# Two experts in 32 slots, and the last expert's rows added to the sums by VectorE

## The chip, the cores and the metric

The kernel runs on one core of a Trainium2 chip. The metric is device microseconds of one execution. TensorE (PE, with PEld its weight loads) multiplies, VectorE (DVE) and ScalarE (ACT) work element by element, GpSimd (POOL) issues indirect and small DMAs, SyncE (SP) issues the weight loads. A difference of under about 0.2% can't be told from no change.

## What is computed

Two layers of a token mixer followed by a channel mixer, on 256 latent and 256 context tokens of 1024 features, in float32. The second layer's channel mixer is the part in question: each of 256 tokens goes to its best two of eight experts.

```python
def moe_swiglu(h, router, w1, w3, w2):
    logits = (h @ router).astype(jnp.float32)
    top_vals, top_idx = lax.top_k(logits, TOP_K)        # TOP_K = 2
    top_w = jax.nn.softmax(top_vals, axis=-1)
    gates = jnp.sum(jax.nn.one_hot(top_idx, N_EXPERTS, dtype=jnp.float32) * top_w[..., None], axis=-2)
    out = jnp.zeros_like(h)
    for e in range(N_EXPERTS):                          # w1, w3: 1024 x 2816; w2: 2816 x 1024
        out = out + gates[..., e:e + 1].astype(h.dtype) * swiglu(h, w1[e], w3[e], w2[e])
    return out
```

Here swiglu(h, w1, w3, w2) is (silu(h @ w1) * (h @ w3)) @ w2. Its sum is normalised, multiplied by a gate and added to the tokens: the output.

## The kernel before

The trunk (first layer, second layer's token mixer) is not touched by the change. The experts run in `experts`, in the order of RUNS (line 35), each on a fixed number of token slots, SLOTS (line 33). Position 0 is always expert 0; positions 1 to 7 are the other experts by falling load (lines 1499 to 1513). An expert with more tokens than slots is finished in a loop behind the output (line 1605), under a condition that is false as long as all tokens fit.

An expert's weights are 33 tiles of 128 x 2048 float32, 1 MiB each: in `up` six chunks of up to 512 columns of w1 and w3 (four tiles a chunk, the last chunk of 256 columns two), in `down` eleven tiles of w2. `wload` (line 164) issues them on SP's queue, in the order of use, into a rotating set of 13 buffers; before the first expert starts, six more tiles go to memory lent by other buffers. A tile is issued when the buffer before it in the rotation has been read.

Products come in two kinds. A group of 128 slots splits each weight tile on ScalarE and VectorE into a high and a low part (`wsplit`, line 175) and uses three fast products for one (`mm3`, line 232). A smaller group of m slots uses plain float32 products, which the trace records as two each, with the group's features as the stationary operand, m columns wide, and 128/m such products on different column groups of the array (lines 1336 to 1341 and 1365 to 1369). For 64 slots a product of `up` has 256 weight columns and two column groups, for 32 slots 128 and four; in `down` 512 and two, or 256 and four. In the chunk of 256 columns both forms have 128 columns and two column groups. Behind each chunk `act` multiplies the two halves and transposes the result on TensorE (line 1306), once per 128 columns of it.

While a run computes, `ready` prepares the next: `index` finds the tokens by a small product (line 1223), `fetch` gets their rows by an indirect DMA from `xrows`, which was stored at line 1544 in run 0, and `gather` transposes them (line 1278). Each step of it is placed behind one more chunk. `scatter` writes an expert's results to `yrows`. For the last run it is different: its results don't go through memory. `add_up` reads all others' results back and adds them; `last_sums` loads these sums into four PSUM banks by a product with the identity (line 1394); `combine` scales the last expert's results, splits them and adds them to the same banks by products with a one-hot matrix; `output` reads the banks.

Of the kernel before, what the change touches and what calls it, by code (L numbers as in the profile page):

```python
# [10 lines left out]
F32 = mybir.dt.float32  # L11
F32R = mybir.dt.float32r
I32 = mybir.dt.int32
AF = mybir.ActivationFunctionType
OP = mybir.AluOpType
# [14 lines left out]

SLOTS = (64, 160, 128, 128, 64, 64, 64, 64)

RUNS = ((0,), (2,), (4,), (1, 6), (5,), (3,), (7,))
SCRATCH = 4096
RING2, RING3 = 3, 6
MA = 3
# [7 lines left out]
def shape_constants():  # L46
# [5 lines left out]
    c[:, C_I8:C_I8 + 8] = np.arange(8)  # L52
    c[:, C_CAP:C_CAP + 8] = SLOTS
    p = np.arange(128)
# [27 lines left out]
def finish(steps):  # L82
    for _ in steps:
        pass
# [12 lines left out]
class Net:  # L97
# [1059 lines left out]
    def experts(self, pool):  # L1157
        nc, I = self.nc, self.I
        v = nc.vector
# [3 lines left out]
        onesr = pool.tile([128, 128], F32R, name="onesr", tag="G", bufs=1)  # L1163
        tri = pool.tile([128, 128], F32R, name="tri", tag="GT", bufs=1)
        v.tensor_copy(onesr, self.ones)
# [23 lines left out]
        for t in range(2):  # L1189
            for s in range(t + 1):  # L1190
                nc.tensor.matmul(p[:, t * 8:t * 8 + 8], lhsT=tri if s == t else onesr, rhs=sel[:, s],
                                 start=s == 0, stop=s == t)
# [8 lines left out]
        pieces = []  # L1201
# [55 lines left out]
            return xr, few  # L1257

        def group(n):
            return pool.tile([128, 4, 8 * n], F32, name="few", tag=f"few{n}", bufs=1 + n // 64)  # L1260

        def gather(base, n, rk=None, w=None, got=None):

            xr, few = got or (None, None)
            if xr is None:
                P = places("P", base, n, rk, w, 1)
            if n < 128:
                few = few or group(n)
                xs = few[:, 0].rearrange("p (k s) -> p k s", s=n)
            else:  # L1270
                xh = pool.tile([128, KB, 128], F32R, name="xh", tag="xh", bufs=1)
                xl = pool.tile([128, KB, 128], F32R, name="xl", tag="xl", bufs=1)
            for q in range(2):
                p = self.at()
                for k in range(4):
                    d = (4 * q + k) * 128
                    if xr is not None:
                        nc.tensor.transpose(p[:, k * 128:k * 128 + n], xr[:, d:d + 128], self.ident[:n, :n])
                        continue
                    for t in range(2):  # L1280
                        nc.tensor.matmul(p[:, k * 128:k * 128 + n], lhsT=res[t][:, d:d + 128], rhs=P[:, t, :n],
                                         start=t == 0, stop=t == 1)
                xg = xs[:, 4 * q:4 * q + 4] if n < 128 else pool.tile([128, 4, 128], F32, name="xg", tag="xg", bufs=1)
                for k in range(4):
                    kk = 4 * q + k
                    a, b = A[:, 0, kk:kk + 1], B[:, 0, kk:kk + 1]
                    if q:
                        nc.scalar.activation(xg[:, k, :n], p[:, k * 128:k * 128 + n], AF.Identity, scale=a, bias=b)
                    else:
                        v.tensor_scalar(xg[:, k, :n], p[:, k * 128:k * 128 + n], a, b, op0=OP.mult, op1=OP.add)  # L1290
                s = slice(4 * q, 4 * q + 4)
                if n == 128:
                    self.split(xh[:, s], xl[:, s], xg)
            return (xh, xl) if n == 128 else (xs, few)
# [79 lines left out]
                                     f + j == 0, f + j == FB - 1)  # L1374
                yield ys

        def adder(base, n, rk, gt_, last=False):

            p = self.at()
            G = places("G", base, n, rk, None, 1)  # L1380
            for t in range(2):
                nc.tensor.transpose(p[:, t * 128:(t + 1) * 128], G[:, t], self.ident)
            for t in range(2):
                nc.tensor.matmul(p[:, 256:257], lhsT=G[:, t], rhs=gt_(t), start=t == 0, stop=t == 1)
            GT = pool.tile([128, 256], F32R, name="GT", tag="GT", bufs=1)
            nc.scalar.activation(GT, p[:, :256], AF.Copy)
            gcol = pool.tile([128, 1], F32, name="gcol", tag="gcol", bufs=2)
            v.tensor_copy(gcol, p[:, 256:257])
            sums = []
            if last:  # L1390

                sums = [self.at() for _ in pieces]
                for o, a in zip(sums, pieces):
                    nc.tensor.matmul(o, lhsT=self.ident, rhs=a, start=True, stop=False)
            return n, GT, gcol, sums

        def combine(to, y):
            n, GT, gcol, sums = to

            parts = []  # L1400
            ys = pool.tile([128, 4, 512], F32R, name="ys", tag="acts", bufs=MA)
            for i, h in enumerate(y):
                hi, lo = ys[:, 2 * i], ys[:, 2 * i + 1]
                nc.scalar.activation(hi, h, AF.Copy, scale=gcol)
                v.scalar_tensor_tensor(lo, h, gcol, hi.bitcast(F32), op0=OP.mult, op1=OP.subtract)
                parts.append((hi, lo))
            for t in range(2):
                for half in range(2):
                    o = sums[2 * t + half] if sums else self.at()
                    r = slice(0, 128) if n == 128 else slice(64 * half, 64 * half + 64)  # L1410
                    for i, x in enumerate(parts[half % len(parts)]):
                        nc.tensor.matmul(o, lhsT=GT[r, t * 128:(t + 1) * 128], rhs=x[r], start=i == 0 and not sums, stop=i == 1)
                    a = pieces[2 * t + half]
                    if not sums:
                        v.tensor_add(a, a, o)

        def weights(e, static):
            def at_(name):
# [5 lines left out]
        def ready(pos, t):  # L1424


            ns = [min(128, SLOTS[pos] - b) for b in range(0, SLOTS[pos], 128)]
            t[pos] = ns, [], []
# [12 lines left out]
        def last_gate():  # L1441
            g = pool.tile([128, D], F32, name="fgate", tag="xh", bufs=1)
            s = self.gscr[1, 1, 0]
            nc.gpsimd.dma_start(g, bass.AP(tensor=s.tensor, offset=s.offset, ap=[[0, 128], [1, D]]))
            return g

        def output(outs, src, g):
            for t in range(2):
                ss = self.small.tile([128, 1, 2], F32, name="ss", tag="ss", bufs=6)
                for half in range(2):  # L1450
                    c = slice(half * 512, half * 512 + 512)
                    junk = pool.tile([128, 512], F32, name="junk", tag="mg", bufs=2)
                    nc.scalar.activation(junk, src[2 * t + half], AF.Square, accum_out=ss[:, 0, half:half + 1])
                    v.tensor_mul(outs[2 * t + half], src[2 * t + half], g[:, c])
                r = self.scale(ss, D)
                for half in range(2):
                    c = slice(half * 512, half * 512 + 512)
                    v.scalar_tensor_tensor(outs[2 * t + half], outs[2 * t + half], r, res[t][:, c], op0=OP.mult, op1=OP.add)
                    nc.sync.dma_start(self.out[t * 128:(t + 1) * 128, c], outs[2 * t + half])
# [13 lines left out]

        def last_sums():
            pos, = RUNS[-1]
            return adder(0, SLOTS[pos], lambda t: rankp[:, t, pos:pos + 1], lambda t: gatep[:, t, pos:pos + 1], True)

        cur = {}
        first_w = lambda t: w0[:, t:t + 1]
# [2 lines left out]
        with self.behind(self.latest(DVE, ACT)):  # L1482
# [5 lines left out]
            for i in range(2):  # L1488
                o, m, b = sm([128, 2, NE], f"oh{i}"), sm([128, 2, NE], f"ohl{i}"), sm([128, 2], f"best{i}")
# [37 lines left out]
            rankp, gatep = sm([128, 2, NE], "rankp"), sm([128, 2, NE], "gatep")  # L1527
# [28 lines left out]

        for i, run in enumerate(RUNS):
            if i == 1:
                n_over = nc.values_load(overi[0:1, NE:NE + 1], min_val=0, max_val=SEQ)
            if i == len(RUNS) - 1:  # L1560
                fgate = last_gate()
            ups, w2s = [], []
            for pos in run:
                ns, xs, _ = cur[pos]
# [7 lines left out]
            nxt = {}  # L1572
            side = chain(*(ready(pos, nxt) for pos in RUNS[i + 1])) if i + 1 < len(RUNS) else add_up()

            hold = self.behind([] if i else routed)
            for c, aTs in enumerate(zip(*ups)):
# [3 lines left out]
                else:  # L1580
                    hold.close()
                    if i == 0:
                        cur[0][2].append(index(0, 0, SLOTS[0])[1:])
            finish(side)
            last = i == len(RUNS) - 1
            if last:
                to = last_sums()
# [10 lines left out]
        outs = pool.tile([128, 4, 512], F32, name="outs", tag="few64", bufs=2)  # L1598
        outs = [outs[:, i] for i in range(4)]

        output(outs, to[-1], fgate)
        for a, o in zip(pieces, to[-1]):
            nc.scalar.activation(a, o, AF.Copy)

        with self.tc.If(n_over > 0):
            with self.tc.For_i(0, NE, 1) as e:
                n_e = nc.values_load(overi[0:1, bass.ds(e, 1)], min_val=0, max_val=SEQ)
                for base in (0, 128):
                    with self.tc.If(n_e > base):
# [4 lines left out]
                        rk = lambda t: col[:, 0, t]  # L1614
# [145 lines left out]
```

## Time and profile before

| | us |
|---|---|
| median of 3 runs (lowest, highest) | 1521.48 (1519.68, 1522.76) |
| the profiled execution, its own time | 1520.14 |
| its span, first to last instruction | 1517.9 |
| TensorE busy | 1452.5 |
| the experts, first up-product to last down-product | 804 to 1502 |

The stages of the experts, from the order of instructions: run 0 (position 0, 64 slots) 804 to 872.6, run 1 (position 2, 128 slots) to 975, run 2 (position 4, 64) to 1046, run 3 (positions 1 and 6, 128 + 32 and 64) to 1259, run 4 (position 5, 64) to 1330, run 5 (position 3, 128) to 1432.5, run 6 (position 7, 64) to 1502, then the output to 1518. Busy time counts an engine's instructions; it doesn't say who waits for whom. The page's granted clock is a share of TensorE's full 2.4 GHz; 1.2 GHz is the other level.

### The profile page before, as it was taken

What the parts mean: (1) busy time and instruction counts of PE and PEld (TensorE: products, weight loads), DVE (VectorE), ACT (ScalarE), POOL (GpSimd) and SP (SyncE); (2) the same over time, 40 slices, a digit from 0 to 9 for tenths busy, and PEclk for the clock granted to TensorE, in tenths of its full rate; (3) what the DMA queues carried; (4) which work ended last, traced back from release to release, by engine and by line L of the source; (5) the groups of instructions that cost most, each with busy time, mean ns of one, the idle gap of its engine ahead of it and who ended that gap; (6) DMA issues with size and microseconds to landing.
All of it is one profiled execution on the core that took longest, in us unless ns stands there. A gap on an engine that the chain in (4) does not pass through costs nothing.

```text
span 1517.9 us, 22725 instructions
## 1 busy us (share of the span) xinstructions
PE 1452.5 (96%) x9006; PEld 1053.9 (69%) x9007; DVE 823.6 (54%) x1551; ACT 616.4 (41%) x983; POOL 62.5 (4%) x93
## 2 busy tenths in 40 slices
PE   7999999999999999999998999999999998999996
PEld 5677667988878888788665477764666655477762
DVE  3496687774554545778763088622454341078612
ACT  4336654423222222456641177522343331177511
POOL 1010200000000001000000010000000001010000
PEclk9999999999999999999999999999999999999998
DMA  8773223344453525353379899999998899999994
GB/s 340 278 285 146 86 98 123 141 170 163 142 206 135 207 100 186 119 186 111 118 293 420 351 416 368 370 403 419 419 355 329 326 363 393 420 421 409 409 420 180
DMA packets 62995, 410.82 MB, mean 271 GB/s; under 512 B 9428, under 2 KB 10136, under 8 KB 15648
## 3 DMA queue, kind: packets, MB, share of 16 engines
q1 hardware_dynamic: 54864, 392.19, 66.1%
q0 software_dynamic: 5616, 16.29, 2.9%
q8 instruction: 73, 1.20, 0.3%
q10 hardware_dynamic: 2400, 0.79, 0.2%
q14 instruction: 42, 0.34, 0.1%
HBM read 402.27 MB, written 6.98 MB: 270 GB/s over the span
## 4 chain that ended last, share of the span: by engine, by line
PE 84%; DVE 6%; DMA 5%; ACT 3%; issue 2%; ACTq 0%; POOL 0%; DVEq 0%; POOLq 0%
PE mm L1339 12%; PE mm L236 11%; PE mm L235 11%; PE mm L237 11%; PE mm L1368 7%; PE at L235 7%; PE at L236 7%; PE at L237 6%; PE md L373 1%; PE at L747 1%; DVE whl L162 1%; DMA more<-yrows 1%; DMA xr<-xrows,src 1%; PE at L724 1%; DMA few<-xrows,src 1%
## 5 line engine op out<-in xcount | busy, mean ns | idle before, releaser
L162 DVE TENSOR_TENSOR whl<-w,whl 128x1024 fp32r<-128x1024 f32 x310 | 374.5, 1223 | 267.6 <-ACT whl L161 259.2
L161 ACT ACTIVATE whl<-w 128x1024 fp32r<-128x1024 f32 x310 | 323.7, 1058 | 294.0 <-PE at L237 174.1
L1339 PE MATMUL mm<-w,few 128*64 128x256 f32 (+2 forms) x2528 | 225.8, 347 | 0.0
L1339 PEld LDWEIGHTS mm<-w,few 128*64 128x64 f32 (+1 forms) x2528 | 147.6, 133 | 68.6 <-issue 17.7
L1368 PE MATMUL mm<-w,few 128*64 128x512 f32 (+1 forms) x616 | 111.2, 536 | 0.0
L235 PE MATMUL mm<-hh,whl 128*128 128x512 f32 (+1 forms) x256 | 95.7, 374 | 1.2 <-ACT hh L161 1.2
L236 PE MATMUL mm<-hl,whl 128*128 128x512 f32 (+1 forms) x256 | 95.9, 375 | 0.0
L237 PE MATMUL mm<-hh,whl 128*128 128x512 f32 (+1 forms) x256 | 95.5, 373 | 0.0
L1368 PEld LDWEIGHTS mm<-w,few 128*64 128x64 f32 (+1 forms) x616 | 35.0, 129 | 70.6 <-issue 68.3
L237 PE MATMUL mm<-whl,hl 128*128 128x256 f32 (+1 forms) x240 | 80.9, 342 | 0.0
L236 PE MATMUL mm<-whl,hh 128*128 128x256 f32 (+1 forms) x224 | 75.3, 338 | 1.8 <-DVE whl L162 1.8
L1303 DVE TENSOR_TENSOR mg<-mg,mm 128x256 f32<-128x256 f32 (+2 forms) x36 | 13.6, 378 | 114.2 <-ACT mg L1302 114.2
L235 PE MATMUL mm<-whl,hh 128*128 128x256 f32 (+1 forms) x224 | 74.8, 338 | 0.0
L236 PE MATMUL at<-hl,whl 128*128 128x512 f32 (+1 forms) x192 | 71.3, 371 | 0.0
L237 PE MATMUL at<-hh,whl 128*128 128x512 f32 (+1 forms) x192 | 71.3, 371 | 0.0
L235 PE MATMUL at<-hh,whl 128*128 128x512 f32 (+1 forms) x192 | 71.2, 371 | 0.0
L367 DVE SCALAR_TENSOR_TENSOR wsum<-w,sc,wsum 128x1024 f32<-128x1024 f32 x48 | 59.7, 1281 | 20.8 <-DMA w<-in_w_mod_dram 20.8
L1302 ACT ACTIVATE mg<-mm 128x256 f32<-128x256 f32 (+3 forms) x54 | 22.8, 422 | 117.7 <-PE mm L1339 113.1
L235 PE MATMUL mm<-whl,xh 128*128 128x512 f32 (+1 forms) x144 | 57.9, 402 | 7.5 <-ACT whl L161 7.5
L236 PE MATMUL mm<-whl,xh 128*128 128x512 f32 (+1 forms) x144 | 57.2, 397 | 2.8 <-DVE whl L162 2.8
L235 PEld LDWEIGHTS mm<-hh,whl 128*128 128x128 f32 x256 | 48.2, 188 | 11.3 <-issue 2.1
L237 PE MATMUL mm<-whl,xl 128*128 128x512 f32 (+1 forms) x144 | 55.6, 386 | 0.0
(492 smaller groups left out, 2604.1 us busy)
## 6 DMA issues: line engine op xcount, KB each, us to landing
w<-in_moe_w_dram SPq DMA_DIRECT2D x258, 1024.0 KB, 11.5
w<-in_w_mod_dram SPq DMA_DIRECT2D x48, 1024.0 KB, 6.0
w<-in_ffn_w_dram SPq DMA_DIRECT2D x33, 1024.0 KB, 4.9
w<-in_w_in_dram SPq DMA_DIRECT2D x16, 1024.0 KB, 4.9
w<-in_w_out_dram SPq DMA_DIRECT2D x8, 1024.0 KB, 5.5
wa<-in_moe_w_dram SPq DMA_DIRECT2D x3, 1024.0 KB, 9.7
gate<-gscr POOLq DMA_DIRECT2D x5, 512.0 KB, 4.8
band<-in_band_dram SPq DMA_DIRECT2D x4, 512.0 KB, 7.8
```

The lines of the kernel that those rows point to most:

```text
L161: self.nc.scalar.activation(hi, x, AF.Copy)
L162: self.nc.vector.tensor_sub(lo, x, hi.bitcast(F32))
L235: mm(out, lhsT=a[0], rhs=b[0], start=start, stop=False)
L236: mm(out, lhsT=a[0], rhs=b[1], start=False, stop=False)
L237: mm(out, lhsT=a[1], rhs=b[0], start=False, stop=stop)
L367: nc.vector.scalar_tensor_tensor(x, y, c, x, op0=OP.mult, op1=OP.add)
L373: nc.tensor.matmul(p[32 * j:32 * j + 32], lhsT=self.sc[:, k], rhs=w[:, 0, j * 512:(j + 1) * 512], start=k == split, stop=k == KB - 1 and n ...
L724: nc.tensor.matmul(sp[:, :n], lhsT=qT[:, h, t * 128:t * 128 + 128], rhs=kT[:, kv, j, c0:], start=j == 0, stop=j == 1)
L747: nc.tensor.matmul(op[64 * i:64 * i + 64, side * 256:side * 256 + 256], lhsT=vt[:, b + 2 * side, kv * 64:kv * 64 + 64], rhs=src[:, b], sta ...
L1302: nc.scalar.activation(s1[:r, :c], h1[:r, :c], AF.Silu)
L1339: nc.tensor.matmul(h[i][m * j:m * j + m, :c], lhsT=x[0][:, k], rhs=t[:, k - k0, j * c:j * c + c], start=k == 0, stop=k == KB - 1, tile_pos ...
L1368: nc.tensor.matmul(y[0][m * q:m * q + m, :c], lhsT=x[0][:, b], rhs=w[:, j, c * q:c * q + c], start=f + j == 0, stop=f + j == FB - 1, tile_ ...
```

## The change

SLOTS gives 32 slots instead of 64 to positions 0 and 7. RUNS pairs position 7 instead of 6 with position 1 in run 3, and position 6 instead of 7 runs last. The 32-slot buffers (`few32`) become two; the scratch tile of a 128-row gather takes its memory from the ring of `mg` instead of one of its own. In the last run the sums stay in SBUF: `combine` scales the results in two halves, ScalarE one and VectorE the other, places them by one plain float32 product for each of four output blocks instead of two split ones, and VectorE adds each block to the sums. `output` then reads the sums, and four copies behind it are gone.

```diff
-SLOTS = (64, 160, 128, 128, 64, 64, 64, 64)
-RUNS = ((0,), (2,), (4,), (1, 6), (5,), (3,), (7,))
+SLOTS = (32, 160, 128, 128, 64, 64, 64, 32)
+RUNS = ((0,), (2,), (4,), (1, 7), (5,), (3,), (6,))
...
-            return pool.tile([128, 4, 8 * n], F32, name="few", tag=f"few{n}", bufs=1 + n // 64)
+            return pool.tile([128, 4, 8 * n], F32, name="few", tag=f"few{n}", bufs=2)
...
-                xg = xs[:, 4 * q:4 * q + 4] if n < 128 else pool.tile([128, 4, 128], F32, name="xg", tag="xg", bufs=1)
+                xg = xs[:, 4 * q:4 * q + 4] if n < 128 else pool.tile([128, 4, 128], F32, name="xg", tag="mg", bufs=2)
...
-            GT = pool.tile([128, 256], F32R, name="GT", tag="GT", bufs=1)
+            GT = pool.tile([128, 256], F32, name="GT", tag="GT", bufs=1)
...
-            sums = []
-            if last:
-                sums = [self.at() for _ in pieces]
-                for o, a in zip(sums, pieces):
-                    nc.tensor.matmul(o, lhsT=self.ident, rhs=a, start=True, stop=False)
-            return n, GT, gcol, sums
+            return n, GT, gcol
...
-            parts = []
-            ys = pool.tile([128, 4, 512], F32R, name="ys", tag="acts", bufs=MA)
+            ys = pool.tile([128, 2, 512], F32, name="ys", tag="acts", bufs=MA)
             for i, h in enumerate(y):
-                hi, lo = ys[:, 2 * i], ys[:, 2 * i + 1]
-                nc.scalar.activation(hi, h, AF.Copy, scale=gcol)
-                v.scalar_tensor_tensor(lo, h, gcol, hi.bitcast(F32), op0=OP.mult, op1=OP.subtract)
-                parts.append((hi, lo))
+                nc.scalar.activation(ys[:, i, :256], h[:, :256], AF.Copy, scale=gcol)
+                v.tensor_scalar(ys[:, i, 256:], h[:, 256:], gcol, None, op0=OP.mult)
             for t in range(2):
                 for half in range(2):
-                    o = sums[2 * t + half] if sums else self.at()
+                    o = self.at()
                     r = slice(0, 128) if n == 128 else slice(64 * half, 64 * half + 64)
-                    for i, x in enumerate(parts[half % len(parts)]):
-                        nc.tensor.matmul(o, lhsT=GT[r, t * 128:(t + 1) * 128], rhs=x[r], start=i == 0 and not sums, stop=i == 1)
+                    nc.tensor.matmul(o, lhsT=GT[r, t * 128:(t + 1) * 128], rhs=ys[r, half % len(y)], start=True, stop=True)
                     a = pieces[2 * t + half]
-                    if not sums:
-                        v.tensor_add(a, a, o)
+                    v.tensor_add(a, a, o)
...
-        output(outs, to[-1], fgate)
-        for a, o in zip(pieces, to[-1]):
-            nc.scalar.activation(a, o, AF.Copy)
+        output(outs, pieces, fgate)
```

## Rows read from the trace of the kernel before

**Rows 1.** The page: busy time and share of the span by engine.
```profile
PE 1452.5 (96%) x9006; PEld 1053.9 (69%) x9007; DVE 823.6 (54%) x1551; ACT 616.4 (41%) x983; POOL 62.5 (4%) x93
```

**Rows 2.** By stretch: us, PE, PEld, DVE, ACT, POOL busy, clock, DMA share, GB/s.
```profile
804.00:872.60 68.60, 64.93 (x500) 36.07 (x499) 13.05 (x69) 11.84 (x27) 1.77 (x2) 0.98 0.94 382
872.60:975.00 102.40, 99.66 (x454) 78.94 (x454) 87.30 (x88) 76.44 (x84) 4.07 (x2) 0.98 0.99 389
...
1046.00:1259.00 213.00, 208.76 (x1823) 135.13 (x1825) 93.28 (x101) 81.26 (x109) 4.96 (x3) 0.99 0.94 363
1259.00:1330.00 71.00, 64.84 (x497) 36.04 (x493) 5.95 (x18) 8.06 (x20) 3.81 (x4) 0.95 1.01 411
...
798.00:1502.00 704.00, 676.74 (x4782) 444.71 (x4782) 304.64 (x426) 269.11 (x361) 25.51 (x20) 0.98 0.97 385
```

**Rows 3.** Whom TensorE waited for, 804 to 1502: us in total, times, longest.
```profile
PE at L1278 <- DMA xr<-xrows,src: 7.9, 2, 5.1
PE mm L235 <- ACT whl L161: 7.5, 4, 2.3
PE at L1306 <- DVE mg L1303: 5.5, 5, 2.7
...
```

**Rows 4.** Whom SP's queue waited for, 804 to 1502.
```profile
SPq L172 <- PE mm L1339: 206.2, 97, 12.7
```

**Rows 5.** Busy time by stretch, columns as in rows 2: the last loads.
```profile
1490.00:1500.00 10.00, 10.00 (x48) 3.31 (x46) 0.00 (x0) 0.00 (x0) 0.00 (x0) 1.00 0.36 147
```

**Rows 6.** Timeline of TensorE: start, us, then the instruction; 32-slot and 64-slot up-products.
```profile
1059.21 1.08 PE L1339 MATMUL mm<-w,few 128*32 128x128 f32 x32
1060.22 0.50 PE L235 MATMUL at<-whl,xh 128*128 128x512 f32 x1
...
1441.71 7.13 PE L1339 MATMUL mm<-w,few 128*64 128x256 f32 x64
1448.77 0.44 PE L1306 MATMUL at<-cst,mg 128*128 128x128 f32 x2
...
1475.84 1.97 PE L1339 MATMUL mm<-w,few 128*64 128x128 f32 x32
```

**Rows 7.** Timeline of TensorE: the 64-slot down-products of run 0.
```profile
853.38 19.10 PE L1368 MATMUL mm<-w,few 128*64 128x512 f32 x88
```

**Rows 8.** Groups by form, run 3: count, busy us, mean ns, idle before.
```profile
L1339 PE MATMUL mm<-w,few 128*32 128x128 f32 x704 | 29.1, 282 | 0.0
...
L1368 PE MATMUL mm<-w,few 128*32 128x256 f32 x176 | 14.2, 387 | 0.0
```

**Rows 9.** Timeline of run 0: store, index, fetch and transposes for the second run.
```profile
807.84 0.75 POOL L1544 DMA_DIRECT2D xrows<-xt  x1 [41.66 <-ACT xt L1543]
...
811.04 0.61 PE L1223 MATMUL at<-facts,P 128*128 128x4 f32 x4
...
821.49 1.02 POOL L1256 DMA_INDIRECT xr<-xrows,src  x1 [12.90 <-DVE P L1213]
...
830.63 1.09 PE L1278 MATMUL at<-cst,xr 128*128 128x128 f32 x8 [2.86 <-DMA xr<-xrows,src]
```

**Rows 10.** DMA issues, 800 to 840: size, median us from issue to landing.
```profile
xrows<-xt POOLq DMA_DIRECT2D x1, 1024.0 KB, 12.1
```

**Rows 11.** Timeline of TensorE in run 4: after a longer wait.
```profile
1286.74 1.97 PE L1278 MATMUL at<-cst,xr 128*128 128x128 f32 x8 [5.08 <-DMA xr<-xrows,src]
1288.64 3.68 PE L1339 MATMUL mm<-w,few 128*64 128x256 f32 x16
```

**Rows 12.** Timeline of run 6 and the tail: sums, scaling, the output's VectorE chain.
```profile
1479.25 3.68 PE L1394 MATMUL at<-macc,cst 128*128 128x512 f32 x8
...
1502.02 0.69 ACT L1404 ACTIVATE ys<-mm,gcol 128x512 fp32r<-128x512 f32 x1 [22.20 <-PE mm L1368]
...
1504.80 1.29 DVE L1454 TENSOR_TENSOR outs<-at,fgate 128x512 f32<-128x512 f32 x2 [1.31 <-ACT junk L1453]
...
1510.39 1.41 DVE L1458 SCALAR_TENSOR_TENSOR outs<-outs,rstd,res 128x512 f32<-128x512 f32 x2
```

More of the change, by code (lines that the diff above doesn't have):

```diff
@@ L1375, in down, with adder @@
                 yield ys
-        def adder(base, n, rk, gt_, last=False):
+        def adder(base, n, rk, gt_):
             p = self.at()
@@ L1388, in adder @@
             v.tensor_copy(gcol, p[:, 256:257])
-            sums = []
-            if last:
-                sums = [self.at() for _ in pieces]
-                for o, a in zip(sums, pieces):
-                    nc.tensor.matmul(o, lhsT=self.ident, rhs=a, start=True, stop=False)
-            return n, GT, gcol, sums
+            return n, GT, gcol
         def combine(to, y):
-            n, GT, gcol, sums = to
-            parts = []
-            ys = pool.tile([128, 4, 512], F32R, name="ys", tag="acts", bufs=MA)
+            n, GT, gcol = to
+            ys = pool.tile([128, 2, 512], F32, name="ys", tag="acts", bufs=MA)
             for i, h in enumerate(y):
-                hi, lo = ys[:, 2 * i], ys[:, 2 * i + 1]
-                nc.scalar.activation(hi, h, AF.Copy, scale=gcol)
-                v.scalar_tensor_tensor(lo, h, gcol, hi.bitcast(F32), op0=OP.mult, op1=OP.subtract)
-                parts.append((hi, lo))
+                nc.scalar.activation(ys[:, i, :256], h[:, :256], AF.Copy, scale=gcol)
+                v.tensor_scalar(ys[:, i, 256:], h[:, 256:], gcol, None, op0=OP.mult)
             for t in range(2):
                 for half in range(2):
-                    o = sums[2 * t + half] if sums else self.at()
+                    o = self.at()
                     r = slice(0, 128) if n == 128 else slice(64 * half, 64 * half + 64)
-                    for i, x in enumerate(parts[half % len(parts)]):
-                        nc.tensor.matmul(o, lhsT=GT[r, t * 128:(t + 1) * 128], rhs=x[r], start=i == 0 and not sums, stop=i == 1)
+                    nc.tensor.matmul(o, lhsT=GT[r, t * 128:(t + 1) * 128], rhs=ys[r, half % len(y)], start=True, stop=True)
                     a = pieces[2 * t + half]
-                    if not sums:
-                        v.tensor_add(a, a, o)
+                    v.tensor_add(a, a, o)
         def weights(e, static):
@@ L1475, in last_sums @@
             pos, = RUNS[-1]
-            return adder(0, SLOTS[pos], lambda t: rankp[:, t, pos:pos + 1], lambda t: gatep[:, t, pos:pos + 1], True)
+            return adder(0, SLOTS[pos], lambda t: rankp[:, t, pos:pos + 1], lambda t: gatep[:, t, pos:pos + 1])
         cur = {}
```

## The prediction

> **What bounds the kernel now.** I read the stage table first, one row per expert run, then the waits of TensorE and of the DMA queue inside that stretch, then single rows in order of time. TensorE is busy 96% of the span [rows 1]. From 798 to 1502 us, where the eight experts run, the DMA engines are busy too: share 0.97, 385 GB/s [rows 2]. So two resources look like bounds, and the waits decide. The list of what TensorE waits for holds gathers, splits and small steps, and no load of an expert's weights at all [rows 3]; the DMA queue, in contrast, waits 206.2 us for up-products of TensorE to give a weight buffer back [rows 4]. TensorE therefore sets the pace, and the weights follow it with a small lead. How small is seen by run. One expert is 33 tiles of 1 MiB, 34.6 MB; at the best rate in the rows, 419 to 421 GB/s, that is 82 us. A 128-slot run takes 102.4 us and lets the lead grow; a 64-slot run takes 68.6 to 71 us and eats it; run 3, two experts in 213 us for 165 us of transfers, fills every buffer and leaves DMA unused (share 0.94, 363 GB/s) [rows 2]. The last weight lands at about 1493.6 (in the slice from 1490 the engines are busy for 0.36 of 10 us [rows 5]), 8.4 us before the last product. TensorE's savings thus turn into time only until the weights' lead is used up: two limits, to be added up separately.
>
> The routing first: counting the router's choices on the reference's inputs gives expert 0 15 tokens and the others 154, 90, 80, 52, 50, 46 and 25. So 32 slots hold expert 0 and the least loaded one, and the overflow loop stays unused.
>
> **Prices of the two forms.** 64-slot up-products: 64 records (one chunk, four weight tiles) in 7.06 us from their start to the next instruction's, 1.77 us a tile [rows 6]. 32-slot: one tile is 32 records, 1.01 us from its start to the next instruction's [rows 6]; there it stands between full-width products. Halving the columns and doubling the column groups that run at once would give 7.06/8 = 0.88 us a tile when nothing of another shape lies between. I take 0.95, with 0.88 and 1.01 as ends. The last half chunk has 128 columns a record in either form and only two column groups in use, so it saves nothing. Down-products: 64 slots, 88 records in 19.1 us, 1.73 us a tile [rows 7]; 32 slots, 176 records in 14.2 us with other shapes between, 1.29 us a tile, and at the 0.88 of the same arithmetic 9.7 us in all [rows 8]. I take 1.0 a tile, 11.0 us, with 9.7 and 12.5 as ends (the latter from 14.2 less some of its interruptions). The transposes of a chunk go from two to one, about 0.17 us a chunk. One rule of the Trainium skill bears on the choice of 0.95: "TensorEngine Tiling (Array Packing)", section Tiling Modes, says that a change of tiling mode drains the array. By it the 1.01 holds a drain that consecutive 32-slot tiles don't pay, the price would be 0.88, and the sum below some 2 us larger; no row of before has two such tiles in succession, so the trace doesn't decide.
>
> **Run 0 (804 to 872.6).** The naive saving is 20 x 0.82 + 8 for the down-products, over 24 us; most of its first part is lost. The second run's rows are fetched on the way: the store of the normalised tokens is issued after ACT's scaling and lands 12.1 us later, which is about 820; the indirect fetch goes out at 821.49 and lands at 830.6, 9.1 us later [rows 9, 10]. TensorE, in order, stands before the transposes of that fetch until 830.63, with 2.86 us idle [rows 9]. After the change it comes there about 8 us earlier (three chunks of 4.2 us instead of 7.4, less a new wait of some 2.5 us for the routing arithmetic after chunk 0, whose index product starts at 811.04 just when chunk 0 ends [rows 9]), but the fetch can't leave before the store has landed. So the restart moves by 0 to 1.5 us, say 0.8, and the wait grows to some 9 us. From the restart on: 8 full tiles x 0.82 = 6.5, transposes 0.5, down-products 8.1 (6.6 to 9.4). A longer wait costs clock: after 5.08 us idle the transposes take 1.97 us against 1.09 and a tile 3.68 us, twice 1.77, the granted clock at its lower level, 1.2 GHz, for a while (0.95 of full speed over that run, 0.98 to 0.99 over others) [rows 2, 9, 11]; I take 1.0 us more than the 2.86 us wait has cost already. Sum: 0.8 + 6.5 + 0.5 + 8.1 - 1.0 = 15 us (11 to 19).
>
> **Run 3 (1046 to 1259).** Its second expert goes from 64 to 32 slots, all of it in TensorE's order: 20 x 0.82 = 16.3 (15.1 to 17.7), transposes 0.8, down-products 11 x 0.73 = 8.1 (6.5 to 9.5). The gather for the run after stays covered: a pair of chunks still takes some 21 us against about 10 for a fetch. Sum 25.2 us (22.4 to 28).
>
> **Run 6 and the tail.** Position 6 takes position 7's place with the same 64 slots: nothing. Loading the sums into PSUM before the last down-products disappears: four float32 products, 3.68 us, in TensorE's order [rows 12]. After the last product the scaling of y, now two halves of 256 columns, can be ready some 0.3 us sooner than its 0.69 us; four plain float32 products of 512 columns follow, 0.86 to 0.92 us each by the same four [rows 12], two at a time if the two row halves overlap. Then four new additions on VectorE at 0.65 each [rows 12], 2.6 us, ahead of a chain of 7.0 us that VectorE works through anyway (1504.80 to 1511.80 [rows 12]). VectorE starts at about 1503.6 instead of 1504.80, so the end moves out by 1.4 us (0.5 to 3). ScalarE's four copies are removed and were on no path. Net gain 2.2 us (0.7 to 3.2). The move of the gather's scratch tile to another buffer ring, the second 32-slot buffer and the third fetch into the split buffers cost nothing that I can find: VectorE and ScalarE are busy 5 to 13 us of 70 in the 64-slot runs [rows 2]; if that cover failed, a wait of a few us like the 2.86 above would be the price.
>
> **The other limit.** From 798 to 1502 the transfers move 704 x 385 = 271 MB [rows 2]. At 420 GB/s this takes 645 us, so the last weight can't land before 1443; gathers and scatters slow some stretches to 380 to 400, which I put at 10 us: 1453. One tile of products (1.8 us) must follow, so TensorE can't end before about 1455, against 1502 now. TensorE's own sum puts its end at 1502 - 15 - 25.2 - 3.7 = 1458. The two limits meet: the lead of the weights would be almost used up, and some of it will be lost in waits. I take off 2 us for that. Forecast: 15 + 25.2 + 2.2 - 2 = 40.4 us, 1520.14 to 1479.7 for the profiled execution; the median of the runs lies 1.3 us above it, so 1481.
>
> **The rivals.**
> - The weights become the bound early. If the busy share, not the rate, is what is free, unused DMA time is 4.1 us in run 0, 1.0 in run 1, 12.8 in run 3, and some 6.6 us at the end, 24 in all [rows 2, 5], less 1.4 in the tail: 1499. For it: the share is 1.01 in the 64-slot run 4. Against it: the same share goes with 389 GB/s in run 1 and 411 in run 4, and no product waits for weights [rows 2, 3]. Chance 0.17, times of 1489 to 1499.
> - Run 0 gives nothing because everything behind the fetch is filled with waits for weights; run 3 and the tail remain: 25.2 + 2.2, 1494. Chance 0.05.
> - Narrow products are no cheaper. A record of 128 columns in the 64-slot form takes 62 ns (32 in 1.97 us [rows 6]); at that price a 32-slot chunk of 128 records takes 7.9 us against 7.06, 4 us more in run 3 and 1.6 in run 0, nothing gained below, 2 us gained in the tail: 1525. Against it: 704 records in 29.1 us, 41 ns each, in this very kernel [rows 8]. Chance 0.02. The Trainium skill has this as a rule, "TensorE: Matmul & The Clock Gate", Back-to-back issue gap: a stream of weight loads and products of 128 columns runs at about 81 ns each. By that, an estimate, 640 records would be 52 us against 35, 17 us lost in run 3 alone; the row's 41 ns doesn't agree.
> - Slower: the overflow loop. It decides at the 33rd token of expert 0 or of the least loaded expert; then an expert runs again in 128 slots behind the output, with no weights loaded ahead: a 128-slot run of 102.4 us and the output's 10 us again [rows 2, 12], some 1595. The counts 15 and 25 speak against it. Chance 0.03.
>
> **How the numbers follow.** The forecast, 1472 to 1489, has 0.73; the rivals 0.17, 0.05, 0.02 and 0.03. Its low end is the weights' limit (1455 and the tail, about 1472), its high end the lower ends of the terms. For 8 in 10 the range takes in half of the first rival: 1472 to 1496. Faster by over 0.2% (about what a measurement of this kernel can tell from no change) in the first three cases, 0.94 with a little taken off; the same 0.02; slower 0.04.
>
> **What would show it.** After the change: run 0 ends near 857 with one wait of about 9 us before the transposes of the fetched rows; run 3 takes about 188 us; 32-slot tiles follow each other every 0.88 to 1.01 us; DMA moves above 400 GB/s in nearly all of the stretch; from the end of the last down-product to the last VectorE instruction 11 us instead of 9.8. I am wrong if TensorE's list of waits gains entries for weights, if run 0 shortens by more than 20 us (the fetch was not what held it), or if run 3 shortens by less than 20 (the price of the form).

## The result

The changed kernel takes 1477.91 us, median of 4 runs (1474.09 to 1483.88), against 1521.91 for the kernel before: ratio 0.9717, 95% interval 0.9681 to 0.9752, 43 us less. The profiled execution took 1476.53 us with a span of 1474.3. 1481 was forecast, 1472 to 1496 the range.

The stages of the changed kernel, by stretch (us, busy PE, PEld, DVE, ACT, POOL with counts, granted clock, DMA share, GB/s; runs 0, 1, 3, 4, the first 10 us of the end of loading, and all experts):

```profile
804.00:860.00 56.00, 40.40 (x908) 32.57 (x907) 12.17 (x74) 11.13 (x28) 1.77 (x2) 0.88 0.99 392
860.00:962.00 102.00, 99.75 (x456) 79.11 (x456) 87.29 (x88) 75.61 (x83) 4.07 (x2) 0.98 1.01 416
...
1031.80:1215.90 184.10, 178.70 (x2228) 130.33 (x2230) 92.63 (x101) 80.47 (x109) 1.90 (x2) 0.99 1.01 414
1215.90:1286.90 71.00, 64.75 (x495) 36.18 (x495) 5.74 (x18) 7.44 (x20) 3.91 (x4) 0.95 1.01 420
...
1450.00:1460.00 10.00, 8.88 (x40) 2.70 (x36) 1.31 (x3) 0.61 (x2) 0.00 (x0) 1.00 0.21 84
...
798.00:1456.90 658.90, 619.55 (x5575) 434.99 (x5573) 301.73 (x424) 265.65 (x361) 20.25 (x20) 0.97 1.00 410
```

Against [rows 2] two stages are shorter: run 0 (68.6 to 56) and run 3 (213 to 184.1). The others keep their length within about 1.5 us. And the DMA column has changed: 385 GB/s over the experts became 410, and in run 3, which had spare time (363 GB/s), it is 414. The weights now come at nearly their full rate (413 to 420 GB/s) in every stage from 860 on.

What TensorE waited for in the changed kernel, 795 to 1470 (us in total, times, longest), answers to [rows 3]:

```profile
PE at L1278 <- DMA xr<-xrows,src: 18.3, 3, 11.0
PE mm L235 <- ACT whl L161: 7.3, 4, 2.3
PE at L1306 <- DVE mg L1303: 7.3, 6, 3.5
...
PE mm L1339 <- issue: 2.6, 3, 1.0
```

The longest wait, for the fetched rows in run 0, went from 2.86 to 11.0 us. No product waits for weights in the list, though transfers run without a pause. How near the weights are shows at the end. Their last load is issued at 1435.07 and lands 19.7 us later (row of the DMA issues):

```profile
1435.07 0.34 SPq L172 DMA_DIRECT2D w<-in_moe_w_dram  x1
...
w<-in_moe_w_dram SPq DMA_DIRECT2D x1, 1024.0 KB, 19.7
```

That is 1454.8. The last product ends at 1456.9, and a last tile takes 1.94 us (rows of e5 below), so TensorE comes to its last tile just when that has landed. In the kernel before the last load, issued at 1475.3, landed 20.5 us later, 6.2 us ahead of the end of the last product. Does TensorE's order still set the time, or do the weights? In this execution the two ends coincide; what a further saving is worth, the experiments tell.

Run 0, TensorE (and POOL's two steps), in order of time, answers to [rows 7, 9]:

```profile
808.25 0.75 POOL L1533 DMA_DIRECT2D xrows<-xt  x1 [43.21 <-ACT xt L1532]
...
822.12 1.02 POOL L1256 DMA_INDIRECT xr<-xrows,src  x1 [13.12 <-DMA xrows<-xt]
...
818.11 2.83 PE L1339 MATMUL mm<-w,few 128*32 128x128 f32 x96
831.93 1.97 PE L1278 MATMUL at<-cst,xr 128*128 128x128 f32 x8 [11.00 <-DMA xr<-xrows,src]
...
849.53 9.70 PE L1368 MATMUL mm<-w,few 128*32 128x256 f32 x176
```

The fetch is now released by the store of the tokens itself (13.12 us idle, ended by that store), where it was released by VectorE before. TensorE has finished the third chunk at 820.9 and stands until 831.93, no earlier than the 830.63 of before. Behind that point it needs 27.4 us instead of 41.9.

Run 3, TensorE: up-products and down-products with two groups in 32 slots next to each other, and below them the same place of the kernel before, where a 64-slot group stood between:

```profile
1070.90 1.95 PE L1339 MATMUL mm<-w,few 128*32 128x128 f32 x64
1072.79 0.33 PE L1306 MATMUL at<-cst,mg 128*128 128x128 f32 x1
1073.05 2.83 PE L1339 MATMUL mm<-w,few 128*32 128x128 f32 x96
1075.81 0.61 PE L1223 MATMUL at<-facts,P 128*128 128x4 f32 x4
...
1175.93 1.93 PE L1368 MATMUL mm<-w,few 128*32 128x256 f32 x32
1180.79 1.93 PE L1368 MATMUL mm<-w,few 128*32 128x256 f32 x32
```
```profile
1216.21 2.94 PE L1368 MATMUL mm<-w,few 128*64 128x512 f32 x24
1222.08 2.94 PE L1368 MATMUL mm<-w,few 128*64 128x512 f32 x24
```

Three tiles in a row take 2.76 us from their start to that of the next instruction, 0.92 each; with the shape changing around it one took 1.01 [rows 6]. The step between two pairs of down tiles fell from 5.87 to 4.86 us.

The tail answers to [rows 12]:

```profile
1456.93 0.47 ACT L1396 ACTIVATE ys<-mm,gcol 128x256 f32<-128x256 f32 x1 [18.73 <-PE mm L1368]
1457.44 0.48 DVE L1397 TENSOR_SCALAR ys<-mm,gcol 128x256 f32<-128x256 f32 x1 [19.05 <-ACT ys L1396]
1457.98 1.99 PE L1402 MATMUL at<-ys,GT 64*128 64x512 f32 x8 [1.08 <-DVE ys L1397]
1459.14 0.69 DVE L1404 TENSOR_TENSOR macc<-macc,at 128x512 f32<-128x512 f32 x1 [1.22 <-PE at L1402]
...
1467.27 1.41 DVE L1447 SCALAR_TENSOR_TENSOR outs<-outs,rstd,res 128x512 f32<-128x512 f32 x2
```

From ScalarE's scaling to the last VectorE instruction's end it is 11.75 us, 9.78 before. The two halves of the scaling, meant for two engines side by side, run one after the other; the eight records of the four products take 1.99 us, so the row halves do overlap.

### The profile page after: what moved, and what is told of

Read it like the earlier page. It is cut to its first block, busy times and chain, and to the rows that moved or that the text cites. A ratio compares the mean times of both kernels' runs of the same rounds, so it can differ in the third digit from the quotient of the medians.

```text
span 1474.3 us, 24328 instructions
## 1 busy us (share of the span) xinstructions
PE 1395.1 (95%) x9804; PEld 1044.0 (71%) x9805; DVE 823.3 (56%) x1555; ACT 611.2 (41%) x979; POOL 57.3 (4%) x93
## 5 line engine op out<-in xcount | busy, mean ns | idle before, releaser
L1339 PE MATMUL mm<-w,few 128*32 128x128 f32 (+2 forms) x3072 | 197.8, 318 | 2.6 <-issue 2.6
L1339 PEld LDWEIGHTS mm<-w,few 128*32 128x32 f32 (+1 forms) x3072 | 140.4, 124 | 53.1 <-issue 18.9
L1368 PE MATMUL mm<-w,few 128*32 128x256 f32 (+1 forms) x792 | 90.0, 452 | 0.0
L1368 PEld LDWEIGHTS mm<-w,few 128*32 128x32 f32 (+1 forms) x792 | 34.7, 119 | 50.8 <-issue 41.5
L1302 ACT ACTIVATE mg<-mm 128x128 f32<-128x128 f32 (+3 forms) x54 | 21.7, 403 | 101.1 <-PE mm L1339 95.9
L1303 DVE TENSOR_TENSOR mg<-mg,mm 128x128 f32<-128x128 f32 (+2 forms) x36 | 12.2, 339 | 90.9 <-ACT mg L1302 90.8
L235 PEld LDWEIGHTS mm<-hh,whl 128*128 128x128 f32 x256 | 48.2, 188 | 11.1 <-issue 2.1
L235 PE MATMUL at<-whl,xh 128*128 128x512 f32 (+1 forms) x144 | 55.6, 386 | 0.0
```

The source lines that it names most:

```text
L235: mm(out, lhsT=a[0], rhs=b[0], start=start, stop=False)
L1302: nc.scalar.activation(s1[:r, :c], h1[:r, :c], AF.Silu)
L1303: v.tensor_mul(s1[:r, :c], s1[:r, :c], h3[:r, :c])
L1339: nc.tensor.matmul(h[i][m * j:m * j + m, :c], lhsT=x[0][:, k], rhs=t[:, k - k0, j * c:j * c + c], start=k == 0, stop=k == KB - 1, tile_pos ...
L1368: nc.tensor.matmul(y[0][m * q:m * q + m, :c], lhsT=x[0][:, b], rhs=w[:, j, c * q:c * q + c], start=f + j == 0, stop=f + j == FB - 1, tile_ ...
```

## The experiments

Two theories. One: TensorE's order of work sets the time in both kernels, and the parts add up. The other: in the changed kernel the rate of the weights sets it. Ratios are to the kernel before, with their 95% intervals; 0.001 is 1.5 us.

**The parts alone.** e1_tail is the kernel before with the new `adder`, `combine` and `output`. The other two take the changed kernel's memory, the old tail, and

```diff
 e2_run3
+SLOTS = (64, 160, 128, 128, 64, 64, 64, 32)
+RUNS = ((0,), (2,), (4,), (1, 7), (5,), (3,), (6,))
 e3_run0
+SLOTS = (32, 160, 128, 128, 64, 64, 64, 64)
+RUNS = ((0,), (2,), (4,), (1, 6), (5,), (3,), (7,))
```

> The kernel before with the new tail alone (sums left in SBUF, plain float32 products, additions on VectorE). By the theory that TensorE's order sets the end: 3.7 us less ahead of the last down-products, 1.9 us more behind them (11.8 us from the last product to the last VectorE instruction instead of 9.8), so 1.8 us less, a ratio of 0.9988. By the rival that the last weights set the start of those products: no gain ahead, 1.9 us more, ratio 1.0012.

Measured: 0.9989 (0.9977 to 1.0000), as expected from TensorE's order, though the interval touches no change.

> The changed kernel with position 0 back at 64 slots and the old tail, so that only run 3 and its partner differ. Theory: 29 us less, all of it in run 3 (213 to 184 us), ratio 0.981. Rival (weights bound early): run 3 shortens by 15 us or less, or a later run grows by what run 3 saves.

Measured: 0.9785 (0.9773 to 0.9798), 33 us; run 3 took 187 us between the two points where ScalarE starts to scale the results of the run before it and its own last ones (1045.44 to 1232.58; the runs below are measured by the same points). That is 27 us less than before, not 29; run 5 was 2.1 us shorter too, and no later run grew.

> The changed kernel with only position 0 in 32 slots: position 7 back at 64, the old order of runs, the old tail. Theory: 12 to 13 us less, all in run 0, with a wait of about 11 us for the fetched rows; ratio 0.992. Rival (run 0 depends on the weights): under 5 us, since run 1 then waits for weights.

Measured: 0.9916 (0.9894 to 0.9937), 13 us; the wait for the fetched rows was 11.8 us. In its profiled execution TensorE's clock stood at the lower level while it was busy all the time:

```profile
802.00:814.00 12.00, 12.00 (x110) 10.83 (x112) 4.15 (x34) 3.90 (x8) 0.28 (x1) 0.50 0.79 313
```

**The old tail.** e4_oldtail is the changed kernel with `adder`, `combine` and `output` of the kernel before.

> The changed kernel with the old tail. If TensorE's order sets the end here too: 1.8 us slower than the changed kernel, ratio to the kernel before 0.9729. If the last weights set the end (they land within 5 us of the last product), loading the sums costs less than its 3.7 us and the old tail, shorter by 1.9 us behind, is as fast or faster: 0.9705 to 0.9717. Its saving should equal those of the two parts alone, 29 + 12.5 us, if the parts don't share a limit; less by 5 us or more if they do.

Measured: 0.9721 (0.9709 to 0.9734), 42.5 us. It can't be told from the changed kernel, so in this company the new tail is worth nothing that shows. Its trace has what TensorE's order says: the last run is 3.7 us longer (71.9 against 68.2) and the tail 1.95 shorter. The parts e2 and e3 sum to 45.5 us, the whole has 3 less: the sign that a shared limit gives, but the intervals would allow none.

**Work taken from TensorE.** In e5_product the second run's rows come from SBUF by products, and the wait of 11 us goes.

```diff
 e5_product
-                    due.append((n, fetch(n, at[0])))
+                    due.append((n, fetch(n, at[0]) if pos != RUNS[1][0] else None))
...
-                t[pos][1].append(gather(0, n, got=got))
+                rk = (lambda t: rankp[:, t, pos:pos + 1], lambda t: rs[:, t:t + 1]) if got is None else ()
+                t[pos][1].append(gather(0, n, *rk, got=got))
```

> The changed kernel, but the second run's rows are taken from SBUF by one-hot products (32 records of 128 columns, some 5 us of TensorE) instead of the indirect fetch, so that the wait of 11 us in run 0 is gone. If TensorE's order alone sets the end: 11 us and some 2 us at the lower clock less, 5 us more, so about 8 us faster than the changed kernel, ratio to the kernel before 0.966. If the weights' rate is the other limit (420 GB/s from 860 to 1450 in the changed kernel): 0 to 4 us faster, 0.969 to 0.972, and a later run grows by the rest or lists waits for weights.

Measured: 0.9741 (0.9720 to 0.9761): no gain at all. But the edit did a second thing, which its expectation doesn't name. The experts' first loads are issued in another order there, and before the experts start no load is issued for some 14 us. Share and GB/s from 770 to 790, first in the changed kernel, then in e5:

```profile
770.00:790.00 20.00, 19.35 (x135) 13.36 (x133) 11.61 (x34) 8.87 (x22) 0.00 (x0) 1.00 0.84 330
...
770.00:790.00 20.00, 19.03 (x132) 13.05 (x132) 11.60 (x35) 9.60 (x23) 0.00 (x0) 1.00 0.38 137
```

That is 3.9 MB less, 9 us at 420 GB/s, so e5 shows what late weights do and can't decide between the theories alone. The up-products after the wait did start 9 us earlier (824.66 instead of 833.84). Yet run 0 ended only 2.5 us earlier (scatter at 856.83 against 859.30): its down-products, 9.7 us of work, took 17.5. At the kernel's end TensorE takes one tile of w2 every 2.5 us, each released by its load (timeline of TensorE; in brackets the idle time and what ended it):

```profile
1449.51 1.94 PE L1368 MATMUL mm<-w,few 128*64 128x512 f32 x8 [0.65 <-DMA w<-in_moe_w_dram]
1451.90 1.94 PE L1368 MATMUL mm<-w,few 128*64 128x512 f32 x8 [0.45 <-DMA w<-in_moe_w_dram]
1454.49 1.94 PE L1368 MATMUL mm<-w,few 128*64 128x512 f32 x8 [0.65 <-DMA w<-in_moe_w_dram]
```

1 MiB in 2.5 us is 420 GB/s. The waits for weights that the forecast named as its sign are there, though the late start has a share in them.

The same was asked by leaving out down-products, first in e6_cut_after and e7_cut_before:

```diff
 e6_cut_after, e7_cut_before
-        def down(w2, aT, ns):
+        def down(w2, aT, ns, half=False):
...
                     for a, y, m in zip(aT, ys, ns):
+                        if half and j and f + j < FB - 1:
+                            continue
```

(and `i == 2` handed to it). The cut went further than its expectation says: in a 128-slot group the inner loop uses the name `half` too and sets it, so from the first block on the odd blocks were left out in runs 1, 3 (position 1) and 5 as well. By their records that is some 55 us of TensorE instead of 8.7 (180 products of 0.23 us in the 128-slot groups and the 32-slot ones beside them, besides run 2); in the 128-slot groups the splits on VectorE (two of 1.22 us a tile) keep part of it.

> The changed kernel without 10 of the 22 second-half down-product pairs' work in run 2 (position 4): every odd block of w2 but the last is left out, 8.7 us less of TensorE, all weights still loaded. TensorE's order alone: 8.7 us faster than the changed kernel, 0.966. Two limits: 1 to 5 us faster, 0.9685 to 0.971, and the last product ends within 3 us of the last weight.

Measured: 0.9715 (0.9690 to 0.9741). Much more work was left out than meant, and the time is that of the changed kernel. Run 3 fell from 184 to 170 us and run 1 from 102 to 97, but run 4 grew from 71 to 85 and run 6 from 68 to 78. From the first up-product to the end of the last product e6 takes 652.8 us, the changed kernel 652.4. TensorE's waits from 1199 to 1460:

```profile
PE mm L1339 <- DMA w<-in_moe_w_dram: 16.3, 20, 2.0
PE mm L1370 <- DMA w<-in_moe_w_dram: 9.8, 18, 0.6
```

> The kernel before with the same part of run 2's down-products left out. Run 3 gives the weights time to fill every buffer here, so both theories say 8.7 us less, ratio 0.9943; much less would say that the weights bound the kernel before too.

Measured: 0.9828 (0.9809 to 0.9847), 26 us less. Neither theory's number was made for this cut; the kernel before turns some 26 us of it into time, and then run 6 (76 instead of 70 us) waits for weights there too.

The cut as it was meant, with another name for the argument (`skip`), run 2 alone:

> The kernel before without the odd blocks of w2 but the last in the down-products of run 2 alone: 8.7 us less of TensorE, all weights loaded. TensorE sets the pace: 8.7 us faster (7 to 10), ratio 0.9943. Weights set it: no change.

Measured: 0.9936 (0.9915 to 0.9958), 9.7 us (6.4 to 12.9). In its profiled execution run 2 is 6.3 us shorter (64.5 instead of 70.8), and the stretch from the first up-product to the end of the last product 5.1 us (692.9 instead of 698.0).

> The changed kernel with the same cut in run 2 alone. Weights set the end: 0 to 3 us faster than the changed kernel, 0.970 to 0.972, and what run 2 saves appears in later runs. TensorE's order: 8.7 us faster, 0.966.

Measured: 0.9699 (0.9669 to 0.9729), 2.7 us below the changed kernel's ratio. The two intervals together are too wide to shut out 8.7 us; the trace does it. TensorE now waits for weights (first line; 3.7 us of it in run 2, which gets 3.0 us shorter and not 8.7), and each of its last six tiles is released by its load:

```profile
PE mm L1370 <- DMA w<-in_moe_w_dram: 6.8, 10, 1.5
...
1456.31 1.94 PE L1370 MATMUL mm<-w,few 128*64 128x512 f32 x8 [0.46 <-DMA w<-in_moe_w_dram]
1458.88 1.94 PE L1370 MATMUL mm<-w,few 128*64 128x512 f32 x8 [0.64 <-DMA w<-in_moe_w_dram]
```

From the first up-product (808.43) to the end of the last product it takes 652.4 us, the same as the changed kernel. The same 8.7 us of TensorE are worth 5 to 10 us in the kernel before and nothing in the changed one. This pair and e6 decide: in the kernel before TensorE's order sets the time; in the changed kernel it has come down to the weights, whose last load lands 650.3 us after the first up-product with and without the cut (651.0 in e4, 651.1 in e10), and further work taken from TensorE buys nothing.

**Four more loads.** In both kernels one more tile of w2 is loaded, and read by nobody, ahead of the down-products of runs 1, 2, 4 and 5.

```diff
 e8_loads_after, e9_loads_before
-        def down(w2, aT, ns):
+        def down(w2, aT, ns, extra=False):
+            if extra:
+                self.wload(w2(0), 2, D)
```

> The changed kernel with four more weight tiles of 1 MiB loaded and read by nobody, one ahead of the down-products of runs 1, 2, 4 and 5: 4.2 MB, 10 us at 420 GB/s, no work for an engine. Weights set the end: 10 us slower than the changed kernel (8 to 12), some 1488, ratio to the kernel before 0.978. TensorE's order sets it: within 2 us of the changed kernel, 0.972.

Measured: 0.9785 (0.9757 to 0.9813), some 10 us above the changed kernel's ratio. From the first up-product the last load lands 9.8 us later than in the changed kernel, the last product ends 9.8 us later (662.2 us), and each of the last six tiles is released by its load.

> The kernel before with the same four loads. TensorE sets its pace: run 3 has time for the two loads ahead of it, those of runs 4 and 5 (5 us) come out of the 6.6 us that the last weight lands early: 0 to 3 us slower, ratio 1.000 to 1.002. Weights set it: 10 us slower, 1.0066.

Measured: 1.0046 (1.0026 to 1.0066), 7 us, between the two. By ratios this pair isn't clean. In both kernels the two 128-slot runs with an extra load grew by 3 to 4 us each (e9: runs 1 and 5 from 102.1 and 102.5 to 106.2 and 106.6), and not for lack of rate: in e9's run 1 loads landed in about 5 us around that point, so nothing queued. There TensorE waits longer for ScalarE's splits (1.4 us at 942.57), and the granted clock is 0.79 behind it (945 to 950; 1.00 in the kernel before). In e9 that is all: its last load lands 7.6 us before the end of the last product. In e8 the same delays stand in TensorE's order, but its end is set by the loads. So the pair agrees with the one above.

**The spread.** The changed kernel's runs lie 10 us apart, e2's 1.3. The kernel before can spread as far: its 21 executions beside e8, e9, e11 and e12 took 1519.16 to 1530.77.

```diff
 e10_wide
+                        m = max(n, 64)
-                        nc.tensor.matmul(p[:, k * 128:k * 128 + n], lhsT=res[t][:, d:d + 128], rhs=P[:, t, :n],
+                        nc.tensor.matmul(p[:, k * 128:k * 128 + m], lhsT=res[t][:, d:d + 128], rhs=P[:, t, :m],
```

> The changed kernel, but the one-hot products that gather the first expert's tokens have 64 columns instead of 32 (the other 32 are copies that nobody reads). Theory: the spread of the changed kernel, 1474 to 1484 us, comes from TensorE's clock, which stands at 1.2 GHz for up to 13 us around these narrow products in some executions; with 64 columns it stays as in the kernel before: spread under 3 us, median 1474 to 1476. Rival: the spread comes from elsewhere (transfers, the trunk): still some 10 us wide, median 1478.

Measured: 0.9718 (0.9697 to 0.9738), 1473.9 to 1480.9. The spread stays, so the width of these products isn't its cause. Where it arises can be read from the profiled executions. In the changed kernel, e4, e6, e10 and e12 the first up-product starts between 801.0 (e10) and 808.4 (e12); from there to the end each takes 672.0 to 673.1 us. So in these five the difference lies ahead of the experts: the one-hot products start at 797.4 to 801.6, and take 3.7 to 6.9 us. Those of e10, e12 and e11 (the kernel before with a cut in run 2, so 64 columns), and the clock in the latter:

```profile
797.43 3.68 PE L1282 MATMUL at<-P,res 128*128 128x64 f32 x32
...
801.63 6.88 PE L1281 MATMUL at<-P,res 128*128 128x32 f32 x32
...
799.09 6.93 PE L1281 MATMUL at<-P,res 128*128 128x64 f32 x32
...
800.00:804.00 4.00, 4.00 (x21) 4.00 (x21) 1.36 (x9) 0.00 (x0) 0.00 (x0) 0.50 1.01 422
```

The lower clock comes with 64 columns as well as with 32. Over whole executions time and mean granted clock go together: in e10 from 1473.86 us at 0.983 to 1480.93 at 0.977. What lowers the clock in one execution and not in another stays open.

No version beat the changed kernel by more than its interval.

## Why the prediction was right

**What bounds the kernel before: shown.** e11 turned 8.7 us less of TensorE's work into 9.7 us less of time (5.1 in its trace). The row that the prediction read it from doesn't show it: the DMA queue's wait for up-products, 206.2 us [rows 4], is still the longest in the changed kernel, where the weights come at full rate (804 to 1457):

```profile
SPq L172 <- PE mm L1339: 174.6, 87, 11.7
```

The lead of the weights was misread too. The last load landed 6.2 us before the last product, not 8.4; the busy share of a slice is a mean over 16 engines and doesn't say when the last of them is done.

**Run 0: 15 us forecast, 13.7 measured** (68.5 to 54.8 from the first up-product to the scaling of its results). The loss of the first part of its saving came as described: the fetch can't pass the store, the wait grew from 2.86 to 11.0 (some 9 were forecast). The restart moved 1.3 us out (0.8 against the first up-product), not 0.8 in: the store left 0.4 us later and took 0.8 longer (12.9 us), so that the fetch left 0.6 later, and the fetch took 0.7 longer (9.8 us). Behind it 14.5 us were saved (14.1 forecast net); the down-products took 9.70 us, the low end, not the 11.0 chosen.

**Run 3: 25.2 forecast, up to 28; 29.5 measured** (1045.47 to 1259.26 before, 1031.65 to 1215.95 after). The mechanism was right, the price of a 32-slot tile was put too high. The down term gave 11 x 1.01 = 11.1 instead of 8.1: I priced the new group alone, at 1.0 a tile, and it costs 0.93, and the 32-slot group of position 1 next to it became cheaper too, because no other shape stands between them any longer. The up-products gave 17.1 instead of 16.3 (for one chunk, position 1's last tile and the four of position 7 take 1.89 and 2.76 us together; before, the last tile took 1.01 and the four of position 6 7.06). So the price at the low end, 0.88, was nearer than the middle. The Trainium skill says in "TensorEngine Tiling (Array Packing)", section Tiling Modes, that a change of mode drains the array. The trace agrees with what follows from it for tiles in a row, 0.92 and 0.88 against 1.01 alone; that the drain is what the difference consists of isn't shown. The third rival took another figure of the Trainium skill, some 81 ns a product of 128 columns in a stream ("TensorE: Matmul & The Clock Gate", Back-to-back issue gap), for every record. Here 96 records took 2.76 us, 29 ns each, but the records of the column groups overlap (282 ns each, 41 ns from one to the next [rows 8]), so the two can't be compared.

**Run 6 and the tail: 2.2 us forecast, about nothing measured in the whole** (1.7 us in e1 alone, with an interval of 0 to 3.5). Loading the sums is gone, but run 6 is shorter by 1.5 us, not 3.7: the wait of the transposes for VectorE, which adds up the others' results there, grew to 3.5 us (2.7 before), and the products behind it took 1 us longer. Changed kernel, then before:

```profile
1423.69 0.69 PE L1306 MATMUL at<-cst,mg 128*128 128x128 f32 x2 [3.53 <-DVE mg L1303]
1424.31 9.61 PE L1339 MATMUL mm<-w,few 128*64 128x256 f32 x80
...
1466.39 0.55 PE L1306 MATMUL at<-cst,mg 128*128 128x128 f32 x2 [2.69 <-DVE mg L1303]
1466.87 8.67 PE L1339 MATMUL mm<-w,few 128*64 128x256 f32 x80
```

The tail grew by 1.9 us, 1.4 forecast. The missing half us: the halves of the scaling follow each other, 1.0 us instead of some 0.4.

**The other limit: shown, and the two met.** TensorE's own sum put the end of the products at 1458, the weights' floor at 1455; they ended at 1456.9, and the floor came to 1456.8 (the last load at 1454.8 and one tile). No product waited for weights, so the 2 us taken off for that weren't lost in the profiled execution. That nothing more could be had from TensorE the prediction didn't say; e12 and e6 show it. Part of the good total is luck. Run 3 saved 4.3 us more than forecast and the 2 us weren't needed; run 0 gave 1.3 us less, run 6 with the tail 2.6 less.

**The rivals.** The first one, weights that bind early at 1489 to 1499, fell: it took the idle share of DMA for all that was free. The rate went from 385 to 410 GB/s at a share that only rose from 0.97 to 1.00. That run 0 gives nothing fell with e3, the price of narrow products with run 3. The overflow loop didn't run.

**The signs.** Run 0 was to end near 857 (859), run 3 to take 188 (184), the rate to be above 400 in nearly all of the stretch (392 in run 0, 413 and more behind it), 11 us behind the last product (11.75). The list of waits has no weights in it. That is right for this execution, and it doesn't say that the weights' lead is used up: one more cut, and the entries are there (e12).

## What to carry to other kernels

When two resources are both near full, work out for each what it alone would allow, and forecast with the later end; then test which one binds by taking work from one of them, since a list of waits shows what was late, not what would be late next. See that the edit of such a test leaves the other resource as it was. Where executions spread, compare traces from a mark behind the part that isn't under test. A saving in front of an ordered wait for a memory round trip is lost up to that wait; count only what stands behind it. Price narrow tensor products by rows with the same shape on both sides, and recount the neighbours whose surroundings change.

## What was not expected of the hardware

- TensorE's clock can stay at 1.2 GHz while TensorE is busy without a gap: 12 of 12 us at a granted 0.50 in e3, on products of 32 columns and on 32-slot up-products. With 64 columns in the same place it was 1.00 in the kernel before and 0.50 in e11 (800 to 804, 4.00 of 4 us busy).
- Transfers counted as busy at a share of 0.99 moved 389 GB/s in run 1 of the kernel before [rows 2] and 416 in the changed one at 1.01. The share is no measure of what is left.
